# Loads begun singly, a conversion held in one layer, early products at a mixer's head, and a router's lead-in in a fixed order

## Chip, cores and metric

The kernel runs on one core of one Trainium2 chip. The metric is the device time of one execution in microseconds (us). The core has TensorE (PE in the rows, with PEld for its weight loads), VectorE (DVE), ScalarE (ACT), GpSimd (POOL) and SyncE (SP), which issues most of the DMAs.

## What is computed

The reference is a network for 256 tokens of width 1024 in float32: two hybrid layers, an RMS norm, a mixer of four branches, and a mixture of experts with a layer norm. Cut to its frame:

```python
def hybrid_layer(x, c, ...):                    # twice
    mod = silu(c) @ ada_w + ada_b               # six vectors that scale and shift
    h = rms_norm(x, norm_mix_g) * (1 + sc_m) + sh_m
    proj = h @ w_in                             # NA, MLA and GQA inputs, three gates
    o_na = neighborhood_attention(qa, ka, va, na_rpb)
    q_b = rms_norm(cq, mla_q_norm_g) @ mla_w_uq           # the up-projections
    kv_b = rms_norm(ckv, mla_kv_norm_g) @ mla_w_ukv
    o_mla, o_gqa = blocked_attention(...), blocked_attention(...)
    merged = sigmoid(ga) * (o_na @ w_br_na) + ...         # three branches
    x = x + g_m * (merged @ w_out)
    h = rms_norm(x, norm_ffn_g) * (1 + sc_f) + sh_f
    gate, up = split(h @ ffn_w_gate_up)
    return x + g_f * ((silu(gate) * up) @ ffn_w_down)

x = rms_norm(x, final_norm_g)
proj = x @ w_in                                 # mixer: four branches
y_a = rg_lru(a_in, ...)                         # a convolution, then a scan
y_b = gated delta rule on qkv, beta, decay      # "gdn"
y_c = stick-breaking attention; y_d = gated linear attention   # "sb", "gla"
x = layer_norm(a * x + merged @ w_out)
scores = sigmoid(x @ w_router)                  # 16 experts in 4 groups, top 2
x = layer_norm(a * x + sum over chosen experts of weight * expert(x))
```

## The kernel before

Activations stand transposed: features on the 128 partitions, the 256 tokens along the free axis, so that a tile of 1024 features is eight blocks of 128x256. Every large product is done at near float32 precision by three matmuls: each operand is kept as a high part (hi: tiles `wh`, `hh`) and a rest (lo: `wl`, `hl`), and `mm3` (or `blockT`, L195 to L197) issues hi x hi, lo x hi and hi x lo into the same PSUM bank.

A weight reaches PE in three steps. `raw` (L156) has SyncE load 1 MB into one of three raw slots (`wr`); `pieces` has ACT convert each half to the high part (L163) and DVE subtract it from the raw weight to give the rest (L170), each a pass of 128x1024. There are five slots for high parts and five for rests. A raw slot is free for the next load when its conversions and subtractions are done. `pieces` takes three switches: `s.behind` names an instruction after which the conversion must be placed, `s.hold` is a list of instructions after which the next subtractions must be placed, one each, and `s.defer` collects subtractions to be emitted later. Those are orders in the program's sequence, not waits on a value.

The order on each engine comes from a planner, which goes through the program in the order of the code, simulates the engines and lets an instruction pass others where its operands and slots are there. `s.after(a, b)` sets an order by hand. Every engine then works through its own list in order.

**Modulation (`ada`, L385; `tick`, L410).** The six vectors of a layer are sums over products of a row with weights: 8 loads of 512 KB a vector, issued by GpSimd (L405) into one of ten `big` slots, and for each one DVE pass with an accumulated sum (L398). The generator is advanced once per weight load (`tick`, called in `raw`), and with `pace` 2 it issues two loads and does two sums a tick; the sums run four loads behind. In each layer the loads of vectors 4, 3 and 2 begin at the two up-projection weights and go on through the twelve gate weights.

**Attention and up-projection (L735 to L815).** Neighbourhood attention's scores are computed; the exponentials (L134) run on ACT, the sums' reciprocals (L438) and the scaling (L440) on DVE. The program then takes the up-projections: `w_uq` and `w_ukv` are loaded and converted with `s.behind = evac`, the copy that empties a bank of values (L734). PE's products for the query heads are emptied by DVE into `qf` (L768). GpSimd copies keys (`kg`, L788), and the gate weights follow (`L_att.wr`, `L_gates.wr` in the rows: the label is that of the part which was last named), PE's gate products mixed with the attention's steps. After them come the branch products, whose banks DVE empties with L817, and the output product.

**The mixer's head (L1018, L1070, L1486).** `final_norm` ends the norm (`norm_end`, whose reciprocal root is done by `rsq` on ACT and one Newton step on DVE, L252 to L254), keeps the factor r in a slot for weight rests, and scales the input in eight blocks (L1028), each followed by its split into hi and lo (L237 on ACT, L238 on DVE). Two products don't wait for that: they take `s.z`, the input before the factor, and the factor is applied to the product: the two blocks of `rg` (L1487 to L1492, the second one's weight loaded there), and `misc` (L1070, a product of 128 columns, emptied with the factor at L1072). The six gdn products (L1076) use the normalised input; the first is block 2. PSUM banks are named: mm, s and t have two buffers, o and ad one.

**The router's lead-in (L1695 to L1850).** `out_norm` computes the output product by column block i and token half b, with the layer norm's statistics, and starts the router's product from it before the norm is applied. At the last block of each half it makes mr and u (L1715, L1716), and applies the norm in four quarters, each with two DVE passes (L1648, L1649). Then PE adds the carried input into four banks (L1735, `aI` times the normalised rows). `route` completes the scores (L1765), exponential, reciprocal, two rankings, `sel` (L1793); PE counts with `sel` (L1796 to L1799); DVE makes positions and the gather's matrix P (L1841); PE gathers the tokens of each expert (L1854) and goes on to the experts' products. The first expert weights are loaded ahead, and part of their subtractions deferred (`later`). `route_weights` loads `w_rt` at the start into a tile of its own.

## Time and profile before

| | us |
|---|---|
| median of 3 runs | 1578.55 (1578.36 to 1579.76) |
| profiled execution | 1578.81 |
| its span in the trace | 1577.1 |
| PE busy | 1515.9 (96%) |
| DVE busy | 1199.1 (76%) |
| ACT busy | 902.7 (57%) |
| GpSimd busy | 100.7 (6%) |
| mean granted clock of PE | 0.986 of full |

Busy shares are averages over many stages. PE is busy nearly all the time, so the places of interest are those in which it isn't: the table of stretches finds them, and the engines' rows in order of time tell what they waited for. A row of a timeline gives its start, its duration, the engine, the line, the operation, the tile written and those read, a count if like rows were joined, and in brackets the idle time of the engine ahead of it with what ended that.

### The profile page before, as it was taken

The numbers are of one execution on the slowest core, as the hardware profiler recorded it, in microseconds if no ns is written. First come the engines' busy times: TensorE is split into PE (matmuls) and PEld (weight loads), VectorE is DVE, ScalarE is ACT, GpSimd is POOL, SyncE is SP. The second block draws the span as 40 slices with busy tenths as digits, with TensorE's granted clock in tenths as the row PEclk, the third lists the DMA queues.
The fourth block names the chain that finished last, engine by engine and source line by source line (L and its number), as shares of the span: only waits on it lengthen the run. The fifth ranks groups of instructions, "written<-read, shape, count | busy, mean of one in ns | idle before, by whom it ended". The sixth has DMA issues, their size and how long they took to land.

```text
span 1577.1 us, 27664 instructions
## 1 busy us (share of the span) xinstructions
PE 1515.9 (96%) x11216; PEld 1397.5 (89%) x11216; DVE 1199.1 (76%) x1760; ACT 902.7 (57%) x1316; POOL 100.7 (6%) x173
## 2 busy tenths in 40 slices
PE   6999999999997999999998999999999899999996
PEld 5889999999986989999997989989999688888884
DVE  5899789776785997975558875566666798888896
ACT  5565555444563554644446662675555477777774
POOL 0211000000001110000000022122000000000000
PEclk9999999999998999999999999999999999999998
DMA  9879676876446876565554640335656499999992
GB/s 348 283 238 305 198 240 200 308 267 215 134 141 231 288 241 212 183 208 188 187 174 143 188 126 9 117 103 157 186 175 227 160 324 330 330 330 331 332 346 79
DMA packets 206197, 346.27 MB, mean 220 GB/s; under 512 B 6944, under 2 KB 175024, under 8 KB 193776
## 3 DMA queue, kind: packets, MB, share of 16 engines
q1 hardware_dynamic: 191040, 294.42, 56.0%
q0 software_dynamic: 12656, 46.16, 8.3%
q10 hardware_dynamic: 2368, 3.86, 0.7%
q8 instruction: 90, 1.47, 0.4%
q14 instruction: 43, 0.35, 0.1%
HBM read 343.36 MB, written 1.05 MB: 218 GB/s over the span
## 4 chain that ended last, share of the span: by engine, by line
PE 68%; issue 23%; DVE 4%; DMA 3%; ACT 2%; POOL 0%; ACTq 0%; DVEq 0%; POOLq 0%; SPq 0%
PE L_gu.mm L195 5%; PE L_gu.mm L197 5%; PE L_gu.mm L196 5%; PE L_att.mm L195 3%; PE L_att.mm L197 3%; PE L_att.mm L196 3%; PE M_merge.mm L197 2%; PE M_merge.mm L195 2%; PE M_merge.mm L196 2%; PE L_gu.s L196 2%; PE L_gu.s L195 2%; PE L_gu.s L197 1%; PE L_gu.t L197 1%; PE L_gu.t L196 1%; PE L_gu.t L195 1%
## 5 line engine op out<-in xcount | busy, mean ns | idle before, releaser
L197 PE MATMUL L_gu.mm<-L_fnorm.hh,L_gu.wl 128*128 128x256 f32 x640 | 179.0, 280 | 0.0
L196 PE MATMUL L_gu.mm<-L_fnorm.hl,L_gu.wh 128*128 128x256 f32 x640 | 178.8, 280 | 0.0
L195 PE MATMUL L_gu.mm<-L_fnorm.hh,L_gu.wh 128*128 128x256 f32 x640 | 178.1, 279 | 0.0
L170 DVE TENSOR_TENSOR E_gu.wl<-E_gu.wr,E_gu.wh 128x1024 fp32r<-128x1024 f32 x124 | 150.1, 1224 | 21.2 <-ACT E_gu.wh L163 16.8
L170 DVE TENSOR_TENSOR L_gu.wl<-L_gu.wr,L_gu.wh 128x1024 fp32r<-128x1024 f32 x84 | 102.7, 1224 | 70.8 <-ACT L_gu.wh L163 70.3
L163 ACT CAST E_gu.wh<-E_gu.wr 128x1024 fp32r<-128x1024 f32 x124 | 129.7, 1054 | 40.0 <-PE E_gu.mm L197 11.7
L163 ACT CAST L_gu.wh<-L_gu.wr 128x1024 fp32r<-128x1024 f32 x84 | 88.2, 1050 | 112.4 <-PE L_gu.mm L196 70.5
L195 PEld LDWEIGHTS L_gu.mm<-L_fnorm.hh,L_gu.wh 128*128 128x128 f32 x640 | 120.2, 188 | 0.4 <-ACT L_fnorm.hh L310 0.4
L197 PEld LDWEIGHTS L_gu.mm<-L_fnorm.hh,L_gu.wl 128*128 128x128 f32 x640 | 120.5, 188 | 0.0
L196 PEld LDWEIGHTS L_gu.mm<-L_fnorm.hl,L_gu.wh 128*128 128x128 f32 x640 | 120.0, 188 | 0.0
L398 DVE SCALAR_TENSOR_TENSOR ada.big<-ada.big,L_mlaup.crow 128x1024 f32<-128x1024 f32 x80 | 95.9, 1218 | 0.0
L163 ACT CAST L_down.wh<-L_down.wr 128x1024 fp32r<-128x1024 f32 x48 | 50.5, 1052 | 75.3 <-PE L_gu.mm L196 39.8
L170 DVE TENSOR_TENSOR L_down.wl<-L_down.wr,L_down.wh 128x1024 fp32r<-128x1024 f32 x48 | 58.4, 1224 | 38.3 <-ACT L_down.wh L163 38.3
L163 ACT CAST L_att.wh<-L_att.wr 128x1024 fp32r<-128x1024 f32 x44 | 46.3, 1052 | 66.2 <-PE L_att.mm L196 35.7
L170 DVE TENSOR_TENSOR E_down.wl<-E_down.wr,E_down.wh 128x1024 fp32r<-128x1024 f32 x64 | 75.7, 1223 | 5.1 <-ACT E_down.wh L163 4.9
L163 ACT CAST E_down.wh<-E_down.wr 128x1024 fp32r<-128x1024 f32 x64 | 66.3, 1057 | 15.7 <-PE E_down.mm L197 6.5
L170 DVE TENSOR_TENSOR M_merge.wl<-M_merge.wr,M_merge.wh 128x1024 fp32r<-128x1024 f32 (+1 forms) x50 | 48.2, 969 | 30.5 <-ACT M_merge.wh L163 30.5
L405 POOL DMA_DIRECT2D ada.big<-in_ada_t x80 | 42.2, 529 | 390.2 <-DVE ada.big L398 200.9
L163 ACT CAST M_merge.wh<-M_merge.wr 128x1024 fp32r<-128x1024 f32 (+1 forms) x50 | 41.9, 843 | 44.0 <-PE M_merge.mm L196 38.3
L197 PE MATMUL M_merge.mm<-fnorm.hh,M_merge.wl 128*128 128x256 f32 x208 | 59.2, 284 | 0.0
L195 PE MATMUL M_merge.mm<-fnorm.hh,M_merge.wh 128*128 128x256 f32 x208 | 58.1, 279 | 0.0
L196 PE MATMUL M_merge.mm<-fnorm.hl,M_merge.wh 128*128 128x256 f32 x208 | 57.8, 278 | 0.0
(982 smaller groups left out, 5392.0 us busy)
## 6 DMA issues: line engine op xcount, KB each, us to landing
L_gu.wr<-in_w_gu SPq DMA_DIRECT2D x42, 1024.0 KB, 5.1
ada.big<-in_ada_t POOLq DMA_DIRECT2D x80, 512.0 KB, 5.8
E_gu.wr<-in_wu SPq DMA_DIRECT2D x32, 1024.0 KB, 5.1
E_down.wr<-in_wd SPq DMA_DIRECT2D x32, 1024.0 KB, 5.4
E_gu.wr<-in_wg SPq DMA_DIRECT2D x30, 1024.0 KB, 5.0
L_att.wr<-in_w_in SPq DMA_DIRECT2D x22, 1024.0 KB, 6.1
L_down.wr<-in_w_dn SPq DMA_DIRECT2D x22, 1024.0 KB, 4.9
M_merge.wr<-in_w SPq DMA_DIRECT2D x13, 1024.0 KB, 5.3
```

The source lines that it names most:

```text
L163: c = s.nc.scalar.copy(hi, src).ins
L170: i = s.nc.vector.tensor_sub(lo, src, hi).ins
L195: mm(ps, ah, bh, start=first and fresh and k == 0, stop=False, skip_group_check=True)
L196: mm(ps, ah, bl, start=False, stop=False, skip_group_check=True)
L197: mm(ps, al, bh, start=False, stop=last and k == n - 1, skip_group_check=True)
L398: nc.vector.scalar_tensor_tensor(raw, raw, 0.5, s.crow, op0=ALU.mult, op1=ALU.mult, accum_out=sums[:, k:k + 1])
L405: s.tc.keep_in_program_order(nc.gpsimd.dma_start(raw, s.I["ada_t"][l, v, i % 8]))
```

## The change

It has six parts. `ada` takes a new argument `slow`: its first 4 steps give way after every load, and later ones after every second. The conversions of the up-projections are held behind the eviction in layer 0 only. `final_norm` loads the second `rg` weight ahead of the norm's end, and `w_misc` and the weight of gdn's block 2 behind it, their first three subtractions being placed after the Newton step; r gets a tile of its own, and two blocks are split at a time. gdn's block 2 is computed from the input before the factor, in bank t, as misc is, in bank s; `times_zr` applies the factor. A constant mask is computed from another one. In the router's lead-in the norm is applied in halves; for the second token half the second passes are placed by hand, one next to the exponential and one after `sel`, its carry products come after the counts, the copy of its rows is done in halves, and weight subtractions are placed after P. `w_rt` is loaded in the GLA stage, on GpSimd's queue, into a slot that another tile has used.

```diff
-        nc.vector.scalar_tensor_tensor(r, t, -3.0 * n, r, op0=ALU.add, op1=ALU.mult)
+        s.newton = nc.vector.scalar_tensor_tensor(r, t, -3.0 * n, r, op0=ALU.add, op1=ALU.mult).ins
...
-    def ada(s, vs, mods, pace, lag):
+    def ada(s, vs, mods, pace, lag, slow=0):
-            if i % pace == pace - 1:
+            if i < slow or (i - slow) % pace == pace - 1:
                 yield False
...
-        s.side = [s.ada([(l, v) for v in (4, 3, 2)], mods, 2, LAG[0])]
+        s.side = [s.ada([(l, v) for v in (4, 3, 2)], mods, 2, LAG[0], 4)]
-        s.behind = evac
+        s.behind = None if l else evac
...
     def final_norm(s, x):
-        r = s.t([128, 1024], "wl", WH, pool=s.w)[:, :256]
+        r = s.c.tile([128, 256], F32, name="zr")
+        s.ahead = s.ahead, s.load(s.I["w2"][:, 256:512], 8, 256)
         s.norm_end(out=r)
+        s.hold = [s.newton] * 3
+        s.ahead += s.load(s.I["w_misc"], 8, 128), s.load(s.I["w2"][:, OFF["gdn"] + 512:OFF["gdn"] + 768], 8, 256)
...
-            s.split(hi[:, k], lo[:, k], xf[:, k])
+            if k % 2:
+                s.split(*(v[:, k - 1:k + 1].rearrange("p a b -> p (a b)") for v in (hi, lo, xf)))
+    def times_zr(s, p):
+        t = s.t([128, 512], "b2", NB2)
+        v = lambda t: t.rearrange("p (a b) -> p a b", a=2)
+        s.nc.vector.tensor_tensor(v(t), v(p), s.zr.unsqueeze(1).to_broadcast([128, 2, 256]), ALU.mult)
+        return t
...
-        p = s.proj(0, s.z, 128, I["w_misc"])
+        p = s.proj(0, s.z, 128, s.ahead[2], "s")
-        for i, bank in ((2, "mm"), (3, "ad"), (0, "mm"), (1, "o"), (4, "mm"), (5, "ad")):
-            p = s.proj(OFF["gdn"] + 256 * i, x, bank=bank)
+        for i, bank in ((2, "t"), (3, "ad"), (0, "mm"), (1, "o"), (4, "mm"), (5, "ad")):
+            p = s.proj(OFF["gdn"] + 256 * i, *((s.z, 256, s.ahead[3]) if i == 2 else (x,)), bank=bank)
+            if i == 2:
+                p = s.times_zr(p)
...
-            nc.vector.tensor_tensor(s.v4(dm), s.v4(ps), C["mneg"]..., ALU.add)
+            nc.vector.scalar_tensor_tensor(s.v4(dm), C["ugt"]..., -1e30, s.v4(ps), op0=ALU.mult, op1=ALU.add)
...
         for i in range(2):
-            w = s.ahead if i == 0 else s.load(I["w2"][:, 256:512], 8, 256)
             pz = s.acc()
-            s.blocks(pz, w, s.z)
+            s.blocks(pz, s.ahead[i], s.z)
+            p = s.times_zr(pz)
...
         B = s.gla_decay(misc)
+        s.wr = s.t([128, 256], "misc", 1)[:, :128].rearrange("p (k n) -> p k n", k=8)
+        nc.gpsimd.dma_start(s.wr, s.I["w_rt"].rearrange("(k p) n -> p k n", p=128))
...
                     s.norm_stats(st, mv, r, ax[b], b)
+                    scaled(0)
...
-                    for q in range(4):
-                        c = slice(q * 256, (q + 1) * 256)
-                        s.norm_apply(x2, ax[b][:, c], mv, r, g, bb, b, c)
+                    scaled(1)
+                    if b:
+                        s.x2 = shifted
+                    else:
+                        for q in range(2):
+                            shifted(q)
...
-        for b in range(2):
+        def carried(b, i):
             for d in range(2):
                 j = nc.tensor.matmul(yp[2 * b + d], aI, x2[:, b, d * 512:(d + 1) * 512], ...).ins
                 s.after(j, i)
                 i = j
+        carried(0, last[0])
...
         s.fn(sc, u, AF.Exp, scale=-1.0)
+        s.x2(0)
...
+        s.after(s.x2(1), chosen)
...
-        s.after(nc.scalar.copy(xh[:, 1], x2[:, 1]).ins, s.load_ins)
+        s.after(nc.scalar.copy(xh[:, 1, :512], x2[:, 1, :512]).ins, s.load_ins)
...
             if g == 0:
+                nc.scalar.copy(xh[:, 1, 512:], x2[:, 1, 512:])
+                carried(1, at)
                 s.after(nc.vector.tensor_sub(xl[:, 1], x2[:, 1], xh[:, 1]).ins, i)
+                s.placed = i
...
         later, s.defer = s.defer, None
+        s.hold = [s.placed] * 2
...
         for sub in later:
-            sub()
+            s.after(sub().ins, s.placed)
```

`scaled(q)` is the first of the norm's two passes over columns 512q to 512q + 511, `shifted(q)` the second. `chosen` is the instruction that makes `sel`, `at` the last count, and `i`, where `s.placed` is set, the one that makes P.

## Rows read from the trace of the kernel before

**Rows 1.** the page's table of engines: busy time, share of the span, instructions:

```profile
PE 1515.9 (96%) x11216; PEld 1397.5 (89%) x11216; DVE 1199.1 (76%) x1760; ACT 902.7 (57%) x1316; POOL 100.7 (6%) x173
```

**Rows 2.** stretches: length, busy time of each engine, granted clock, DMA share, GB/s:

```profile
80.00:105.00 25.00, 23.00 (x158) 19.79 (x157) 24.19 (x48) 18.00 (x34) 4.70 (x10) 1.00 0.66 219
480.00:505.00 25.00, 13.28 (x98) 11.65 (x97) 11.01 (x22) 7.99 (x16) 5.72 (x12) 0.79 0.83 294
835.00:860.00 25.00, 19.21 (x137) 17.11 (x135) 23.48 (x59) 15.31 (x29) 0.00 (x0) 0.86 0.45 141
1235.00:1260.00 25.00, 18.36 (x98) 13.65 (x97) 21.55 (x61) 10.84 (x17) 0.64 (x2) 0.86 0.53 184
```

**Rows 3.** PE in order of time, layer 1's stall:

```profile
491.38 0.70 PE L426 MATMUL L_att.s<-L_naqkv.big 64*128 64x256 f32 x2
503.58 0.58 PE L195 MATMUL L_mlaup.mm<-L_lat.ch,L_mlaup.wh 128*128 128x256 f32 x1 [11.51 <-DVE L_mlaup.qf L768]
```

**Rows 4.** ACT, DVE, POOL and SP in order of time, the same stall:

```profile
499.98 1.04 ACT L163 CAST L_att.wh<-L_att.wr 128x1024 fp32r<-128x1024 f32 x1 [12.85 <-DMA L_att.wr<-in_w_in]
...
502.06 0.17 DVE L438 RECIPROCAL L_att.psum<-L_att.psum 128x2 f32<-128x2 f32 x1 [10.50 <-ACT L_att.b L134]
...
482.63 3.13 POOL L405 DMA_DIRECT2D ada.big<-in_ada_t  x6
...
483.92 12.70 SPq L156 DMA_DIRECT2D L_att.wr<-in_w_in  x3
```

**Rows 5.** DMAs from 482 to 500: queues; then issues, KB, us to landing:

```profile
q0 software_dynamic: 1152, 4.19, 62.3%
q1 hardware_dynamic: 1784, 1.81, 28.9%
...
ada.big<-in_ada_t POOLq DMA_DIRECT2D x8, 512.0 KB, 7.0
L_att.wr<-in_w_in SPq DMA_DIRECT2D x3, 1024.0 KB, 18.4
```

**Rows 6.** the page's DMA issues of the whole span, us to landing:

```profile
L_att.wr<-in_w_in SPq DMA_DIRECT2D x22, 1024.0 KB, 6.1
```

**Rows 7.** stretches, behind layer 1's stall:

```profile
496.00:508.00 12.00, 4.42 (x20) 4.41 (x21) 3.35 (x11) 4.83 (x14) 0.53 (x1) 0.50 0.76 248
```

**Rows 8.** DVE in order of time, router:

```profile
1244.74 0.87 DVE L1649 SCALAR_TENSOR_TENSOR M_out.x<-M_out.x,lnr,M_out.b 128x256 f32<-128x256 f32 x2
...
1246.55 1.22 DVE L170 TENSOR_TENSOR E_gu.wl<-E_gu.wr,E_gu.wh 128x1024 fp32r<-128x1024 f32 x1
```

**Rows 9.** PE in order of time, mixer's head:

```profile
848.62 0.39 PE L195 MATMUL M_gdn.ad<-fnorm.hh,M_gdn.wh 128*128 128x256 f32 x1 [1.50 <-ACT M_gdn.wh L163]
...
852.95 0.55 PE L195 MATMUL M_gdn.mm<-L_down.hh,M_gdn.wh 128*128 128x256 f32 x1 [3.83 <-DVE M_rg.b L1492]
```

**Rows 10.** DVE in order of time, mixer's head:

```profile
843.41 0.42 DVE L254 SCALAR_TENSOR_TENSOR fnorm.wl<-fnorm.b,fnorm.wl 128x256 f32<-128x256 f32 x1
...
852.12 1.28 DVE L1492 TENSOR_TENSOR M_rg.b<-M_rg.mm,fnorm.wl 128x512 f32<-128x512 f32 x2
```

**Rows 11.** stretches, layer 0's branch products:

```profile
200.00:225.00 25.00, 24.96 (x212) 24.76 (x211) 23.16 (x34) 12.88 (x17) 2.11 (x4) 1.00 0.78 254
```

**Rows 12.** stretches, behind the mixer head's waits:

```profile
853.00:860.00 7.00, 7.00 (x43) 5.79 (x43) 7.00 (x27) 4.95 (x10) 0.00 (x0) 0.77 0.56 185
```

**Rows 13.** PE in order of time, router:

```profile
1241.39 3.26 PE L1735 MATMUL M_ln.s<-M_out.x,M_out.b 128*128 128x512 f32 x4
...
1246.69 1.10 PE L1735 MATMUL M_ln.t<-M_out.x,M_out.b 128*128 128x512 f32 x2 [0.23 <-DVE score L1767]
1250.83 0.18 PE L1796 MATMUL E_route.o<-sel,M_out.b 128*128 128x32 bf16 x1 [3.04 <-DVE sel L1793]
...
1252.45 0.55 PE L1854 MATMUL E_gather.mm<-E_gather.P,M_out.hh 128*128 128x256 f32 x1 [1.38 <-DVE E_gather.P L1841]
```

**Rows 14.** stretches, block 0's carries:

```profile
1242.00:1244.00 2.00, 2.00 (x4) 0.56 (x2) 2.00 (x6) 0.46 (x2) 0.00 (x0) 0.50 0.01 4
```

More of the change, by code (lines that the diff above doesn't have):

```diff
@@ L933, in shape_constants2 @@
     o["ugt"] = (j > i)
-    o["mneg"] = np.where(i >= j, 0, -1e30)
     for b in (1, 2, 4, 8, 16, 32, 64):
@@ L1002, in proj @@
     def proj(s, col0, x, ncol=256, w=None, bank="mm"):
-        w = s.load(s.I["w2"][:, col0:col0 + ncol] if w is None else w, 8, ncol)
+        w = w or s.load(s.I["w2"][:, col0:col0 + ncol], 8, ncol)
         p = s.acc(bank)
@@ L1140, in gdn @@
             dm = s.t([128, 512], "b2", NB2)
-            nc.vector.tensor_tensor(s.v4(dm), s.v4(ps), C["mneg"].unsqueeze(1).to_broadcast([128, 4, 128]), ALU.add)
+            nc.vector.scalar_tensor_tensor(s.v4(dm), C["ugt"].unsqueeze(1).to_broadcast([128, 4, 128]), -1e30, s.v4(ps), op0=ALU.mult, op1=ALU.add)
             for h in range(4):
@@ L1486, in rglru @@
         for i in range(2):
-            w = s.ahead if i == 0 else s.load(I["w2"][:, 256:512], 8, 256)
             pz = s.acc()
-            s.blocks(pz, w, s.z)
-            p = s.t([128, 512], "b2", NB2)
-            v = lambda t: t.rearrange("p (a b) -> p a b", a=2)
-            nc.vector.tensor_tensor(v(p), v(pz), s.zr.unsqueeze(1).to_broadcast([128, 2, 256]), ALU.mult)
+            s.blocks(pz, s.ahead[i], s.z)
+            p = s.times_zr(pz)
             for j in range(2):
@@ L1643, in norm_tiles @@
         return s.t([128, 2, 2, 6], tag + "st", 1), s.t([128, 2, 2], tag + "mv", 1), s.t([128, 2], tag + "r", 1)
-    def norm_apply(s, out, z, mv, r, g, b, t, c):
-        nc = s.nc
-        nc.vector.scalar_tensor_tensor(out[:, t, c], z, mv[:, t, 0:1], g[:, c], op0=ALU.subtract, op1=ALU.mult)
-        nc.vector.scalar_tensor_tensor(out[:, t, c], out[:, t, c], r[:, t:t + 1], b[:, c], op0=ALU.mult, op1=ALU.add)
     def out_norm(s, m, xf):
@@ L1714, in block, with scaled, shifted @@
                     s.norm_stats(st, mv, r, ax[b], b)
+                    half = lambda q: (x2[:, b, q * 512:(q + 1) * 512], ax[b][:, q * 512:(q + 1) * 512], g[:, q * 512:(q + 1) * 512], bb[:, q * 512:(q + 1) * 512])
+                    def scaled(q):
+                        o, z, gq, _ = half(q)
+                        return nc.vector.scalar_tensor_tensor(o, z, mv[:, b, 0:1], gq, op0=ALU.subtract, op1=ALU.mult).ins
+                    def shifted(q):
+                        o, _, _, bq = half(q)
+                        return nc.vector.scalar_tensor_tensor(o, o, r[:, b:b + 1], bq, op0=ALU.mult, op1=ALU.add).ins
+                    scaled(0)
                     nc.vector.scalar_tensor_tensor(mr[:, b:b + 1], mv[:, b, 0:1], -1.0, r[:, b:b + 1], op0=ALU.mult, op1=ALU.mult)
                     nc.vector.scalar_tensor_tensor(u[:, b * 16:b * 16 + 16], s.csbw[:, :16], mr[:, b:b + 1], s.csbw[:, 16:], op0=ALU.mult, op1=ALU.add)
-                    for q in range(4):
-                        c = slice(q * 256, (q + 1) * 256)
-                        s.norm_apply(x2, ax[b][:, c], mv, r, g, bb, b, c)
+                    scaled(1)
[4 more added lines that the diff above has]
+                            shifted(q)
         ws, last = {}, [None]
@@ L1729, in out_norm @@
                 nc.vector.tensor_sub(xl[:, 0], x2[:, 0], xh[:, 0])
-        i = last[0]
         yp = [s.acc(t) for t in "sstt"]
-        for b in range(2):
+        def carried(b, i):
             for d in range(2):
@@ L1737, in out_norm @@
                 i = j
-        return x2, xh, xl, yp, s.route(pr[:, :32], u, r)
+        carried(0, last[0])
+        return x2, xh, xl, yp, s.route(pr[:, :32], u, r) + (carried,)
     def route_weights(s):
-        s.wr = s.c.tile([128, 8, 16], F32, name="wrt")
-        s.late(s.nc.gpsimd.dma_start(s.wr, s.I["w_rt"].rearrange("(k p) n -> p k n", p=128)))
         s.rb = s.c.tile([128, 16], F32, name="rb")
@@ L1792, in route @@
         sel = s.c.tile([128, 32], BF16, name="sel")
-        nc.vector.scalar_tensor_tensor(v4(sel), v4(r), 2.0, gm.unsqueeze(2).to_broadcast([128, 8, 4]), op0=ALU.is_lt, op1=ALU.mult)
+        chosen = nc.vector.scalar_tensor_tensor(v4(sel), v4(r), 2.0, gm.unsqueeze(2).to_broadcast([128, 8, 4]), op0=ALU.is_lt, op1=ALU.mult).ins
         pp = s.acc("o")
@@ L1798, in route @@
         for b in range(2):
-            nc.tensor.matmul(pp[:, 32:48], s.onesb[:, 0], sel[:, 16 * b:16 * b + 16], start=False, stop=b == 1, skip_group_check=True)
+            at = nc.tensor.matmul(pp[:, 32:48], s.onesb[:, 0], sel[:, 16 * b:16 * b + 16], start=False, stop=b == 1, skip_group_check=True).ins
+        s.after(s.x2(1), chosen)
         pos, mx = (s.c.tile([128, n], F32, name=m) for n, m in ((16, "pos"), (1, "most")))
@@ L1808, in route @@
         nc.vector.tensor_reduce(mx, n8, axis=AX.X, op=ALU.max)
-        return sel, sc, pos, mx
+        return sel, sc, pos, mx, at
     def combine(s, sel, sc):
@@ L1823, in moe @@
         ident = s.cst["ident"]
-        sel, sc, pos, mx = rt
+        sel, sc, pos, mx, at, carried = rt
         s.table(SILU)
         LAB[0] = 'E_gather.'
-        s.after(nc.scalar.copy(xh[:, 1], x2[:, 1]).ins, s.load_ins)
+        s.after(nc.scalar.copy(xh[:, 1, :512], x2[:, 1, :512]).ins, s.load_ins)
         f = lambda t: t.rearrange("p a b -> p (a b)")
```

## Prediction

> **What bounds the kernel.** I read the engine table first: TensorE (PE) is busy 1515.9 of 1577.1 us [rows 1], so 61.2 us is all that a better order can give back, apart from matmuls that ran at a low clock. Next comes the table of stretches, and in it the few of 25 us in which PE is far from full: 13.28, 19.21 and 18.36 us busy, which leaves 11.72, 5.79 and 6.64, and a lesser one in layer 0 with 23.00, which leaves 2.00 [rows 2]. Together 26.2 of the 61.2 us. All four lie where the diff works, and in the three large ones the granted clock is under 1 as well. In each I then read the engines in order of time for the wait that ended last. Elsewhere PE is close to full, and what VectorE (DVE) or ScalarE (ACT) saves there is worth nothing.
>
> **Layer 1, the softmax stall.** PE ends its score products at 491.38 + 0.70 = 492.08 and next works at 503.58, after 11.51 idle, released by VectorE's qf (L768) [rows 3]. What ended last stands further back: DVE's reciprocal at 502.06 had waited 10.50 for the exponentials, and these were queued on ACT behind a conversion that had waited 12.85, to 499.98, for a 1 MB gate weight to land. SyncE had issued that weight at 483.92, once a conversion had given a raw slot back; GpSimd had issued six modulation loads of 512 KB in one burst from 482.63 [rows 4]. From 482 to 500 eight modulation loads landed in 7.0 us at the median and three gate weights took 18.4 [rows 5]; over the whole run such gate weights take 6.1 [rows 6].
>
> The change works on both causes in this layer. Without `behind` the up-projection's conversion goes as soon as its weight and a slot are there, no longer after an eviction, so the raw slot comes back sooner. How much sooner the trace of before can't show: nothing, or so much that the weight lands ahead of the burst. And with the first four modulation loads begun one to a tick, three or four are begun by that point and not six. With 6.1 us to land, a weight issued at 483.92 is there at 490.0 even if it is issued no earlier, and its conversion is over at 491.1 (1.04). DVE had stopped at 502.06 - 10.50 = 491.56, so its input to the exponentials was ready. From the end of the conversion to PE's restart it took 503.58 - 499.98 - 1.04 = 2.6; so PE restarts near 491.6 + 2.6 = 494.2, and some 2.1 of the 11.5 remain, about what layer 0 loses in its stretch [rows 2]. That is 9.4. The matmuls behind the stall ran at a granted clock of 0.50 (1.2 GHz): 4.42 us of work from 496 to 508 [rows 7], half of which, 2.2, comes back where PE doesn't stand so long. 9.4 + 2.2 = 11.6; **I take 11**, for weights that are still somewhat late. Bounds: 13.7 (11.5 + 2.2) if nothing is left, 6 if the burst is only halved (rival C).
>
> **Layer 0** keeps `behind`; its loads begin singly too. 2.00 us is all there is; I take 0.4, between 0 and 1.5. Price of beginning singly: the last sums come two weight ticks later (16 for 14), four sums a layer, each a pass of 128x1024, 1.22 by the nearest row of that size [rows 8]. I cost them at nothing, the gate products hide them; without that cover they cost 4 x 1.22 = 4.9 a layer (rival D). No load is added.
>
> **Mixer head.** PE runs dry at 848.62 (1.50) and at 852.95 (3.83, until DVE's L1492 has freed the bank that the misc product needs) [rows 9]. The norm's last Newton step is at 843.41; L1492 comes only at 852.12, behind gains, subtractions and weight subtractions [rows 10]; DVE is busy 23.48 of 25 [rows 2]. The change gives PE products that need no normalised input: misc in bank s, 24 matmuls, which was there but blocked, and gdn's block 2 in bank t, 48 that came later. A full stretch holds 212 such matmuls in 24.96 us [rows 11], 0.118 each; 72 x 0.118 = 8.5, so PE has work from about 847.1 to 855.6. Is DVE ready by then? From 843.8 it owes three held weight subtractions (3 x 1.22), eight gains (8 x 0.42, by the Newton step's 128x256), four subtractions and two scalings of 512 (6 x 0.65, L1492 took 1.28 for two): 3.7 + 3.4 + 3.9 = 11.0, so 854.8. It just fits, and the convolutions wait too. Gain: 5.3 of idle, and the half clock behind it, 7.00 us of work at a mean of 0.77 [rows 12], 1.6; together 6.9. **I take 5**, for a wait of about 2 on the normalised input; bounds 0 (DVE sets the pace, rival B) and 7. The scaling that gdn's block adds costs DVE 0.65, in the stretch counted. zr in a tile of its own gives one lo slot to the weights; three more weights are loaded ahead on SyncE's queue, which pushes the next ones behind the release of their slots: in the wait of 2. The mask that is computed in place of a constant lengthens two operations by a few hundredths: 0.1.
>
> **Router.** PE waits 3.04 for sel at 1250.83 and 1.38 for the gather's P at 1252.45 [rows 13]. In DVE's order a weight subtraction of 1.22 stands ahead of the reciprocal at 1246.55, and before it quarter passes of block 1's normalisation, two in 0.87, which the scores don't need [rows 8]. The change holds such subtractions until P is placed (this one and one like it from further ahead, 2.44), and moves the four second passes (4 x 0.44 = 1.8) as two halves, one beside the exponential, one behind sel. Onto the path come about 0.7 for a scaling ahead of the scores and 0.4 each where a half outlasts what hides it (halves of 512 at 0.65 to 0.7). 2.4 + 1.8 - 1.5 = 2.7 earlier at P, 3.1 at sel. But block 1's carry products, 2 x 1.10 at full clock [rows 13], now stand between sel and the gather: from 1250.83 - 3.1 = 1247.7 and the counts to 1250.1, where P is ready at 1249.8. So the gather starts 2.3 earlier. **I take 2.1.** Bounds: 4 if the gather also runs at the full level, -1 if the held subtractions, three or more of 1.22 now behind P, delay the casts of what was gathered. The load of w_rt goes from the start to the GLA stage on GpSimd's queue: one issue, about 0.5 by the burst (six in 3.13) [rows 4], ahead of GLA's products there; it is needed only after the merges. Nothing.
>
> Here the clock counts. Block 0's four carry rows took 3.26, at a granted clock of 0.50 after PE had had gaps, block 1's four took 2.20 [rows 13, 14]. Behind some 4 us of idle the moved ones may meet the low level themselves; then they end 1.1 later, and the gather behind them comes to the full level sooner, which gives about as much back. That is why the term stays. The Trainium skill's page "TensorE: Matmul & The Clock Gate", Part 1, What's actually happening, speaks against this move: the throttled state is the default, and activity releases it. By that alone the term would be about 1 and the time 1 us longer; the row of that stretch agrees with it, and no row shows these products in their new place.
>
> **The sum.** 11 + 0.4 + 5 + 2.1 = 18.5, less 0.1 for the mask. The profiled execution is its span and 1.7 around it, 1578.81, 0.3 over the median of the runs. 1578.8 - 18.4 = 1560.4, said as **1560**.
>
> **Rivals.**
> A, the forecast: 1560. Chance 0.57.
> B, DVE sets the pace in the head and the router, where it was busy 23.48 and 21.55 of 25 [rows 2] and its work is moved, not taken out: only layers 0 and 1 give, 1578.8 - 11.4 = 1567. For it: the 11.0 us that only just fit. Against: 8.5 us of PE work that waits for no DVE. 0.15.
> C, the burst still meets the gate weights, because GpSimd then sends what has gathered. With four loads in flight for eight, 2.1 of 4.19 MB are spared, at the 6.0 MB in 18 us of that stretch [rows 5] 6.3 us, and the clock gives nothing: 6, and 7.4 elsewhere: 1578.8 - 13.4 = 1565. 0.12. The Trainium skill's page "DMA: Bandwidth & Descriptors", Queues, rings and completion order, says that a DMA engine takes the queues with work in turn, a packet at a time. By that the queue of larger packets gets the larger share, as it does in rows 5, and C would give back somewhat more.
> D, slower: the modulation sums arrive in the branch stage. There DVE is busy 23.16 of 25 with what frees PE's banks, and PE 24.96 [rows 11], so a sum put there is paid in full. It decides from eight sums a layer behind the branch's start: 8 x 1.22 = 9.8, and 2 for the clock, in both layers, 23.6: more than the 18.4 gained, 1584. Against: by ticks only four come later. 0.08.
> E, the diff leaves the order in these stretches as it was, since most of it isn't written by hand: 1577. 0.08.
>
> **Chances and range.** A, B and C are faster by over 0.2% (3.2 us, about what a measurement of this kernel can tell from no change): 0.84. E is the same, 0.08; D is slower, 0.08. Range: A with its terms at 13, 0.5, 7 and 4 gives 1554, at 9, 0, 3 and 1 gives 1566; B and C lie within 1568, both together at 1578.8 - 6.4 = 1572. **1554 to 1572** leaves out D, E and a little.
>
> **What would show it.** Layer 1: no wait of over 4 us on ACT for L_att.wr from 480 to 510, and a clock of 1.00. Head: misc and gdn's block 2 running to about 855, then one wait of 2 at most. Router: sel 3 us sooner after the output projection's last product, block 1's carries right behind it. Against it: ACT at a weight for 10 us (C, E), DVE full and PE waiting for it behind 847 (B), L398 among the branch products (D).

## The result and the profile after

The changed kernel takes 1558.1 us (median of 4 runs, 1557.59 to 1559.87), the kernel before beside it 1579.15 (4 runs, 1578.36 to 1581.09). The ratio is 0.9867, with an interval of 0.985 to 0.9884: faster by 1.3%, clear of the noise, 1.9 us below the 1560 of the forecast and inside its range. The profiled execution took 1558.08, its span 1556.4.

The page's table of engines of the changed kernel, and its table of stretches for the places of rows 2, each at the changed kernel's own times; the columns are those of rows 2:

```profile
PE 1510.9 (97%) x11216; PEld 1392.8 (89%) x11216; DVE 1196.5 (77%) x1749; ACT 901.5 (58%) x1313; POOL 101.7 (7%) x173
```

```profile
80.00:105.00 25.00, 22.97 (x156) 19.57 (x155) 24.05 (x46) 17.99 (x34) 3.91 (x9) 1.00 0.62 205
480.00:505.00 25.00, 24.52 (x188) 21.80 (x188) 19.44 (x37) 15.09 (x32) 6.25 (x13) 1.00 0.88 301
825.00:850.00 25.00, 24.06 (x194) 22.86 (x195) 22.75 (x51) 18.16 (x28) 0.00 (x0) 1.00 0.61 183
1220.00:1245.00 25.00, 18.98 (x93) 13.33 (x92) 21.08 (x55) 11.67 (x20) 0.71 (x2) 0.93 0.59 221
```

PE's idle time has gone from two of the three large places: 13.28 busy of 25 became 24.52 in layer 1, 19.21 became 24.06 in the head, both at a clock of 1.00. The router still has 6.0 idle, and layer 0 is as it was [rows 1, 2]. PE's busy time fell by 5.0 for the same 11216 matmuls, with a mean granted clock of 0.994 where it was 0.986.

Where the 20.7 us of span went is best read from landmarks: the start of the first matmul into a tile that both kernels have, in PE's rows in order of time. The stretches between them, the change against the kernel before in us (start-up ends at layer 0's first L_naqkv.mm, the lead-in is layer 1's norm and modulation up to the same tile there, the stall ends at the first L_gates.mm; the head runs from the first L_gu.mm of layer 1 to M_sbin.mm, the router from the output product's last statistics to E_gu.ad, the tail from there to PE's last matmul; rest: the two stretches between):

| kernel | start-up | layer 0 | lead-in | stall | head | router | tail | rest | all |
|---|---|---|---|---|---|---|---|---|---|
| the change | 1.22 | -0.16 | -1.22 | -10.98 | -7.30 | -1.67 | -0.55 | -0.11 | -20.77 |
| conversion freed alone | -0.15 | -0.12 | -1.24 | -11.76 | 0.41 | 0.15 | -0.04 | 0.02 | -12.73 |
| single loads alone | -0.21 | -0.23 | -1.19 | -1.36 | -0.02 | -0.02 | -0.07 | 0.31 | -2.79 |
| three ticks later alone | -0.46 | -0.11 | -0.51 | -4.98 | 0.00 | 0.08 | -0.05 | -0.30 | -6.33 |
| change, loads in pairs | 0.23 | -0.11 | -1.21 | -11.76 | -7.26 | -2.11 | -0.48 | -0.03 | -22.73 |
| change, no early gdn | 0.24 | -0.10 | -0.25 | -10.98 | -2.43 | -2.11 | -0.34 | 0.08 | -15.90 |
| change, subtractions not held | -0.33 | -0.18 | -0.69 | -10.98 | -7.29 | 2.32 | 0.01 | -0.01 | -17.15 |
| change, once more | 0.50 | -0.20 | -0.16 | -11.00 | -7.27 | -3.25 | -0.46 | -0.05 | -21.89 |

Start-up and lead-in are scatter: programs with the start of the kernel before lie at -0.46 to 2.26, those with the start of the change at -0.33 to 2.58, and the lead-in lies at -1.24 to 1.26. Between programs with the same code the stall repeats to 0.1, the head to 0.4 (the 0.41 of the second line has the head of the kernel before), the router only to 1.6, for a reason that comes below.

### The profile page after: what moved, and what is told of

Its sections match the earlier page's. It is cut to its first block, busy times and chain, and to the rows that moved or that the text cites. A ratio compares the mean times of both kernels' runs of the same rounds, so it can differ in the third digit from the quotient of the medians.

```text
span 1556.4 us, 27649 instructions
## 1 busy us (share of the span) xinstructions
PE 1510.9 (97%) x11216; PEld 1392.8 (89%) x11216; DVE 1196.5 (77%) x1749; ACT 901.5 (58%) x1313; POOL 101.7 (7%) x173
## 4 chain that ended last, share of the span: by engine, by line
PE 68%; issue 23%; DVE 4%; ACT 2%; DMA 1%; POOL 0%; ACTq 0%; POOLq 0%; DVEq 0%; SPq 0%
PE L_gu.mm L195 5%; PE L_gu.mm L196 5%; PE L_gu.mm L197 5%; PE L_att.mm L195 3%; PE L_att.mm L197 3%; PE L_att.mm L196 3%; PE M_merge.mm L197 2%; PE M_merge.mm L195 2%; PE M_merge.mm L196 2%; PE L_gu.s L196 2%; PE L_gu.s L195 2%; PE L_gu.s L197 2%; PE L_gu.t L197 1%; PE L_gu.t L196 1%; PE L_gu.t L195 1%
## 5 line engine op out<-in xcount | busy, mean ns | idle before, releaser
L398 DVE SCALAR_TENSOR_TENSOR ada.big<-ada.big,L_mlaup.crow 128x1024 f32<-128x1024 f32 x80 | 96.3, 1219 | 0.0
L170 DVE TENSOR_TENSOR L_att.wl<-L_att.wr,L_att.wh 128x1024 fp32r<-128x1024 f32 x44 | 53.4, 1220 | 8.4 <-ACT L_att.wh L163 8.2
```

The source lines that it names most:

```text
L170: i = s.nc.vector.tensor_sub(lo, src, hi).ins
L398: nc.vector.scalar_tensor_tensor(raw, raw, 0.5, s.crow, op0=ALU.mult, op1=ALU.mult, accum_out=sums[:, k:k + 1])
```

## The experiments

**The layer 1 stall: which of the two causes?** The theory of the prediction was that both parts work together, the earlier conversion and the smaller burst. The rivals: the conversion alone does it, or the burst alone does. Four kernels tell them apart. The first is the kernel before with the conversion freed in layer 1 and nothing else:

```diff
-        s.behind = evac
+        s.behind = None if l else evac
```

> The kernel before with one edit: in layer 1 the up-projection's conversion is no longer held behind the eviction. Theory 1, late issue: the first gate weight is requested some 9 us sooner, lands ahead of the burst of modulation loads, and ACT waits under 4 us for it; the stall of 11.5 us shrinks to 0 to 2 and the time falls by 11 to 13, to 1566 to 1568. Theory 2, burst alone: the weights still meet six modulation loads, a stall of 6 or more stays, 1572 to 1575.

It took 1566.17, and its stall is 11.76 shorter: the whole of it. The second is the kernel before with its loads begun singly and the conversion still held:

```diff
-        s.side = [s.ada([(l, v) for v in (4, 3, 2)], mods, 2, LAG[0])]
+        s.side = [s.ada([(l, v) for v in (4, 3, 2)], mods, 2, LAG[0], 4)]
```

> The kernel before with one edit: modulation loads begun singly for the first four steps, in both layers. If beginning singly is one of the two causes taken away, as the prediction has it, the burst at 482.6 is three or four loads and the stall falls to about 5: 1572 to 1574. The rival, from the trace of the changed kernel, where five loads still leave in one burst: the burst is one load shorter, a little over 1 us at most is gained, 1577 to 1580.

It took 1576.09, the stall 1.36 shorter, about what the rival said. The third begins layer 1's modulation loads three ticks later, the conversion still held:

```diff
         raws = []
+        for _ in range(wait):
+            yield False
...
-        s.side = [s.ada([(l, v) for v in (4, 3, 2)], mods, 2, LAG[0])]
+        s.side = [s.ada([(l, v) for v in (4, 3, 2)], mods, 2, LAG[0], 3 if l else 0)]
```

> The kernel before with one edit: in layer 1 the modulation loads begin three weight ticks later, so that the burst is one or two loads; the conversion stays held. Theory burst: the gate weight that is requested at 484 lands in about 6 us, at 490, and the stall shrinks to 2 or 3, 1567 to 1570. Theory late issue alone: the stall stays above 8, 1576 or more. Six sums come later, which may cost up to 5 behind the branch's start.

It took 1572.49, the stall 4.98 shorter: between the two theories. ACT, POOL, SP and PE in order of time, of the conversion freed alone, then of the single loads alone and of the later loads alone; "x6" counts joined rows:

```profile
486.42 1.05 ACT L163 CAST L_att.wh<-L_att.wr 128x1024 fp32r<-128x1024 f32 x1
...
481.38 3.14 POOL L405 DMA_DIRECT2D ada.big<-in_ada_t  x6
...
473.50 54.81 SPq L156 DMA_DIRECT2D L_att.wr<-in_w_in  x8
```

```profile
495.48 1.04 ACT L163 CAST L_att.wh<-L_att.wr 128x1024 fp32r<-128x1024 f32 x1 [9.97 <-DMA L_att.wr<-in_w_in]
...
481.00 2.62 POOL L405 DMA_DIRECT2D ada.big<-in_ada_t  x5
...
499.07 0.58 PE L195 MATMUL L_mlaup.mm<-L_lat.ch,L_mlaup.wh 128*128 128x256 f32 x1 [8.64 <-DVE L_mlaup.qf L768]
```

```profile
494.07 1.04 ACT L163 CAST L_att.wh<-L_att.wr 128x1024 fp32r<-128x1024 f32 x1 [8.00 <-DMA L_att.wr<-in_w_in]
...
481.56 2.10 POOL L407 DMA_DIRECT2D ada.big<-in_ada_t  x4
...
497.66 0.58 PE L195 MATMUL L_mlaup.mm<-L_lat.ch,L_mlaup.wh 128*128 128x256 f32 x1 [6.66 <-DVE L_mlaup.qf L770]
```

With the conversion freed, the burst of six is still there, and ACT waits for no weight at all: the gate weights are requested from 473.50 on, 7.9 us ahead of the burst. With the conversion held, the wait follows what GpSimd has sent: 12.85 behind six loads [rows 4], 9.97 behind five, 8.00 behind four. The burst isn't all of it, since single loads follow it while the weight is still on its way. GpSimd's queue from the weight's request to its landing, of the kernel before (483.92 to 499.96), the single loads alone (482.29 to 495.46) and the later loads alone (482.85 to 494.05): packets, MB, share of the 16 engines:

```profile
q0 software_dynamic: 1145, 4.17, 67.7%
...
q0 software_dynamic: 858, 3.12, 63.7%
...
q0 software_dynamic: 711, 2.59, 60.5%
```

That is about eight loads, six and five. All queues together moved 5.98, 4.88 and 4.07 MB in these 16.04, 13.17 and 11.20 us, at 373, 371 and 363 GB/s: the weight is late by the bytes that land with it, at a rate that hardly changes. So what GpSimd has sent is what makes a late weight so late, and the conversion is what makes it late. That is rival C's mechanism, though in the change no wait comes of it: the third gate weight, requested at 488.26 behind its burst, takes 8.8, and ACT waits for no weight. The Trainium skill's page "DMA: Bandwidth & Descriptors", Queues, rings and completion order, has queues served in turn, packet by packet; that the queue of the larger packets (4.17 MB in 1145, against 1.80 in 1769 on the weight's) moved more agrees with it in sign, and no run here isolates packet size.

The fourth is the changed kernel with loads in pairs again (the argument 4 made 0), which asks what beginning singly is worth in it:

> The changed kernel with one part undone: modulation loads begun in pairs again. If the freed conversion alone removes the stall, the time stays within 1 us of the changed kernel, 1557 to 1559. If beginning singly is needed as well, 4 to 6 us of the stall return, 1562 to 1564.

It took 1556.11. The stall is 11.76 shorter than in the kernel before, for 10.98 in the change: beginning singly costs 0.78, in this pair and in every program of either kind. No wait explains it (ACT waits for no weight in either). PE's small attention products stand in another order among the large ones: from start to next start, the 64 of L457 into L_att.o take 8.69 us in the change and 8.11 here, the 64 of L448 7.93 and 7.78. That is 0.73 of the 0.78.

**Layer 0: why is the conversion still held there?** The changed kernel with `s.behind = None` in both layers:

> The changed kernel with one edit: the conversion isn't held in layer 0 either. In layer 1 of the changed kernel the freed conversion stands 1 us ahead of an eviction, whose wait on PE grew from 0.68 to 1.50. Theory: layer 0 has no late gate weight, so it only pays the same 0.8: 1558 to 1560. Rival: the first gate weight comes sooner there too and 0.5 to 1 us of layer 0's 2 us of waits go.

It took 1563.98, worse than theory and rival both; layer 0 is 6.62 longer than in the kernel before. Its ACT, PE and SP rows in order of time:

```profile
74.84 1.04 ACT L163 CAST L_mlaup.wh<-L_mlaup.wr 128x1024 fp32r<-128x1024 f32 x1 [4.65 <-DMA L_mlaup.wr<-in_w_uq]
75.80 0.58 ACT L734 COPY L_naqkv.big<-L_naqkv.mm 128x512 f32<-128x512 f32 x1
...
76.43 0.58 PE L195 MATMUL L_gqaqkv.mm<-L_lat.hh,L_gqaqkv.wh 128*128 128x256 f32 x1 [5.31 <-ACT L_naqkv.big L734]
...
67.21 0.37 SPq L156 DMA_DIRECT2D L_mlaup.wr<-in_w_uq  x1
```

In layer 0 the up-projection's weight is requested only at 67.21. A conversion that is free to go early stands in ACT's list ahead of an eviction, waits 4.65 for its weight, and the eviction, which was ready, and PE behind it wait along (5.31, where the change has 0.68). That is 4.6 of the 6.62; most of the rest is half clock, a granted 0.50 over 3.57 us of PE's work from 76 to 80. In layer 1 the same weight is there (requested at 457.12, converted at 472.02), so there the early place costs little. The same edit is a gain of 11.8 in one layer and a loss of 6.6 in the other.

**The head: are both early products needed?** The changed kernel with gdn's block 2 computed from the normalised input again, in bank t, misc still early:

```diff
-        s.hold = [s.newton] * 3
-        s.ahead += s.load(s.I["w_misc"], 8, 128), s.load(s.I["w2"][:, OFF["gdn"] + 512:OFF["gdn"] + 768], 8, 256)
+        s.hold = [s.newton]
+        s.ahead += s.load(s.I["w_misc"], 8, 128),
...
-            p = s.proj(OFF["gdn"] + 256 * i, *((s.z, 256, s.ahead[3]) if i == 2 else (x,)), bank=bank)
-            if i == 2:
-                p = s.times_zr(p)
+            p = s.proj(OFF["gdn"] + 256 * i, x, bank=bank)
```

> The changed kernel with gdn's block 2 computed from the normalised input again, in bank t, its weight loaded in its turn; misc stays early in bank s. In the trace of the changed kernel misc ran late (at 854.8) and gdn's block 2 alone filled the gap, 834.8 to 840.7. Theory: that block is the cover, 5.7 us of products; without it PE waits for the normalised input, which DVE has two weight subtractions (2.4 us) sooner, so 2 to 4 us are lost, 1560 to 1562. Rival: misc, 2.8 us of products, moves up and is cover enough, within 1 us of the changed kernel.

It took 1562.99, and the head gains 2.43 in place of 7.30. PE in order of time:

```profile
835.74 0.38 PE L196 MATMUL M_gdn.t<-fnorm.hl,M_gdn.wh 128*128 128x256 f32 x1 [0.35 <-DVE fnorm.hl L238]
...
839.27 0.58 PE L197 MATMUL M_gdn.t<-fnorm.hh,M_gdn.wl 128*128 128x256 f32 x1 [3.03 <-DVE M_gdn.wl L170]
```

and the stretch behind it, from 839 to 850:

```profile
839.00:850.00 11.00, 10.73 (x69) 10.06 (x70) 11.00 (x37) 6.99 (x12) 0.00 (x0) 0.75 0.44 127
```

So gdn's block 2 carries 4.9 of the 7.3: 2.4 as idle time (gaps of 3.36 in the head for 0.93 in the change) and, by the rest, 2.5 as half clock. Misc, though allowed early in this program too, doesn't fill the gap. But PE waits only 0.35 for the normalised input here, and 3.03 for the rest of the weight, whose subtraction no longer stands right behind the Newton step (838.00, behind the gains). The edit takes away the early product and that place together, so it isn't shown which of the two is worth the 4.9: the normalised input with the subtraction held early wasn't run. The other half of the question is the bank alone: the kernel before with misc in bank s.

```diff
-        p = s.proj(0, s.z, 128, I["w_misc"])
+        p = s.proj(0, s.z, 128, I["w_misc"], "s")
```

> The kernel before with one edit: the misc product goes into bank s. If the bank was all that kept it from the gap, its 24 matmuls (2.8 us) run within the waits of 1.50 and 3.83 us and the head is 2.5 to 3.5 shorter, 1575 to 1577. If the waits were for the normalised input, PE waits for the next product instead, and the head is shorter by under 1.

It took 1584.61, where a gain was expected (4.2 of what it lies above the kernel before is scatter at the start, in the lead-in and the router; the head itself is 1.57 longer). PE in order of time:

```profile
852.46 0.42 PE L195 MATMUL M_gdn.ad<-fnorm.hh,M_gdn.wh 128*128 128x256 f32 x1 [1.85 <-ACT M_gdn.wh L163]
...
856.80 0.55 PE L195 MATMUL M_gdn.mm<-fnorm.hh,M_gdn.wh 128*128 128x256 f32 x1 [3.70 <-DVE M_rg.b L1492]
```

Both waits of rows 9 are there again, 1.85 for 1.50 and 3.70 for 3.83, the second ahead of a gdn product, which now is what wants bank mm. Misc, in a bank of its own, runs only at 869.60. The wait belonged to the bank and to the place of L1492 in DVE's list, and not to misc.

**The router: what holds the gather?** The profile of the change showed a wait that the prediction hadn't seen, DVE's P behind PE's moved carries. The theory for it: `aI` lies in a buffer of the stage's pool, which passes to P's tile, so P can't be written before the last carry has read it. Rival: P is late because of its place in DVE's list. The changed kernel with `aI` in r's lasting tile, free by then:

```diff
-        aI = s.t([128, 512], "b2", NB2)[:, :128]
+        aI = s.zr[:, :128]
```

> The changed kernel with one edit: the scaled identity of the carry products lies in the tile of the norm's factor, which outlives the stage, and no longer in a stage buffer whose memory P gets. Theory: P's wait of 2.66 us for the carry products goes, the gather starts right behind them (0.6 sooner), and DVE's casts come 2.7 sooner, so that PE's waits of 1.06 and 0.25 behind the gather go too: 1.5 to 2 us less, 1555.5 to 1557. Rival: the carries, 3.6 us at half clock, and DVE's held subtractions set the end anyway: under 0.6.

It took 1559.84, of which 2.39 are the start-up's. DVE and PE in order of time, of the change, then of this kernel, and last DVE's P in the change's second profile:

```profile
1231.41 0.76 DVE L1860 TENSOR_TENSOR E_gather.P<-pos,cst 128x256 fp32r<-128x256 f32 x2 [2.66 <-PE M_ln.t L1753]
...
1227.62 0.18 PE L1814 MATMUL E_route.o<-sel,M_out.b 128*128 128x32 bf16 x1 [2.82 <-DVE sel L1811]
1227.73 3.58 PE L1753 MATMUL M_ln.t<-M_out.x,M_out.b 128*128 128x512 f32 x4
1231.94 0.36 PE L1876 MATMUL E_gather.mm<-E_gather.P,M_out.hh 128*128 128x256 f32 x1 [0.62 <-issue]
```

```profile
1230.44 0.76 DVE L1860 TENSOR_TENSOR E_gather.P<-pos,cst 128x256 fp32r<-128x256 f32 x2
...
1229.21 0.18 PE L1814 MATMUL E_route.o<-sel,M_out.b 128*128 128x32 bf16 x1 [1.19 <-DVE sel L1811]
1229.31 1.96 PE L1753 MATMUL M_ln.t<-M_out.x,zr 128*128 128x512 f32 x4
1231.07 0.87 PE L1876 MATMUL E_gather.mm<-E_gather.P,M_out.hh 128*128 128x256 f32 x4
...
1238.75 0.63 PE L197 MATMUL E_gu.o<-E_gather.wh,E_gather.xgl 128*128 128x512 f32 x1
```

```profile
1230.15 0.76 DVE L1860 TENSOR_TENSOR E_gather.P<-pos,cst 128x256 fp32r<-128x256 f32 x2 [1.03 <-PE M_ln.t L1753]
```

The wait is gone and the gather starts right behind the carries, so it was the buffer. From sel's product to the gather it takes 1.86 us and not 4.32, but 1.6 of that is the clock: block 1's carries took 3.58 there and 1.96 here. In the change's second profile they took 1.96 as well, P waited 1.03, and the way was 2.69; so the buffer is worth 0.8 at the gather. At the end of the stretch no gain is shown: the router is 2.22 shorter than in the kernel before, between the change's two profiles (1.67 and 3.25), with a low phase on the first expert's products (0.63 each at 1238.75).

Next, with that edit kept, the first half of block 1's carries goes ahead of the counts, where PE waits for sel anyway (`first()` is `carried(1, j, (0,))`, with j block 0's last carry):

```diff
         s.x2(0)
+        first()
...
-                carried(1, at)
+                carried(1, at, (1,))
```

> As e6_lasting_ai, and the carry product of the first half of block 1 goes ahead of the counts, into PE's wait for sel. Theory: it takes some 1.0 of idle time, and only one product of 1 to 1.8 us stands between sel and the gather: 1.5 to 2 less than e6_lasting_ai, 1553.5 to 1555.5. Rival: the gather then meets the low clock that the carries had borne, and half of that comes back: 0.5 to 1 less than e6_lasting_ai.

Timed against the kernel before it took 1558.34 (4 runs, 1554.47 to 1560.57), ratio 0.9855 with an interval of 0.9831 to 0.9878; its router is 3.11 shorter than that of the kernel before. Beside the run with the lasting `aI` alone that is 0.9, less than the router's scatter, and the median is that of the change: whether the early half helps isn't told apart. And the changed kernel without the held subtractions:

```diff
-        s.hold = [s.placed] * 2
...
-            s.after(sub().ins, s.placed)
+            sub()
```

> The changed kernel with one part undone: the expert weights' subtractions are no longer placed behind P. Theory of the prediction: they stand in the way of the scores again, 2.44 of DVE time, so that sel comes 1.2 to 2.4 later than in the changed kernel (5.69 after the output norm's last product there), and P with it. Rival: P waits for the carry products anyway, so later scores cost the gather less than 1, and the casts behind the gather come sooner, which gives that back.

It took 1561.67; the router is 2.32 longer than before the change. DVE and PE in order of time:

```profile
1222.50 1.17 DVE L168 TENSOR_TENSOR E_gather.wl<-E_gather.wr,E_gather.wh 128x1024 fp32r<-128x1024 f32 x1
...
1225.94 1.21 DVE L170 TENSOR_TENSOR E_gu.wl<-E_gu.wr,E_gu.wh 128x1024 fp32r<-128x1024 f32 x1
...
1230.43 0.19 PE L1814 MATMUL E_route.o<-sel,M_out.b 128*128 128x32 bf16 x1 [4.87 <-DVE sel L1811]
```

From the output product's last statistics to sel it takes 9.43 here, 5.69 in the change, 10.35 before. The holds give 3.74 of the 4.66, the halves 0.92. Two subtractions stand here between those statistics and sel, and a third of 1.22 a little ahead, at 1219.74: together 3.6.

**All that the runs pointed to, beside the change.** The changed kernel with loads in pairs, the lasting `aI` and the early half, and in the same comparison the changed kernel once more:

> Three edits of the changed kernel that single runs favoured: modulation loads in pairs again, the scaled identity in the tile that outlives the stage, one carry product ahead of the counts. By the stretches of those runs: 0.8 less in layer 1, 1 to 1.5 less in the router, 1555.5 to 1556.5 at the median, against the changed kernel run beside it. Rival: a few us of scatter in the start and the clock behind sel cover that: within 1 us of the changed kernel, intervals that overlap.

> The changed kernel itself, timed in the same rounds as e9_pairs_half_early so that the two can be compared: 1557.5 to 1560, a ratio of 0.985 to 0.988 to the kernel before.

The first took 1555.21 (5 runs, 1554.12 to 1557.34), ratio 0.9848, interval 0.9835 to 0.9862; the second 1557.1 (4 runs, 1555.29 to 1557.2), ratio 0.9856, interval 0.9841 to 0.9871. The 1.9 between the medians is what their parts promise (0.78 in the stall, about 1 in the router), but the intervals overlap: that it is faster than the change isn't shown.

## Why the prediction came out as it did

**Layer 1: 11 forecast, 10.98 measured, though the step was wrong in four terms that cancel: luck.** The changed kernel's POOL, SP, ACT and PE rows in order of time, to be read beside rows 3 and 4:

```profile
482.72 2.61 POOL L405 DMA_DIRECT2D ada.big<-in_ada_t  x5
...
474.84 50.38 SPq L156 DMA_DIRECT2D L_att.wr<-in_w_in  x8
...
487.76 1.05 ACT L163 CAST L_att.wh<-L_att.wr 128x1024 fp32r<-128x1024 f32 x1
...
473.60 0.39 PE L195 MATMUL L_gqaqkv.mm<-L_norm.hh,L_gqaqkv.wh 128*128 128x256 f32 x1 [1.50 <-ACT L_naqkv.big L734]
491.20 0.38 PE L195 MATMUL L_mlaup.mm<-L_lat.ch,L_mlaup.wh 128*128 128x256 f32 x1 [0.21 <-DVE L_mlaup.qf L768]
```

and the DMA view of the changed kernel from 470 to 482, ahead of the burst (KB each, us to landing):

```profile
L_att.wr<-in_w_in SPq DMA_DIRECT2D x2, 1024.0 KB, 5.3
```

The failed step is "the change works on both causes". I had the gate weight requested at 483.92 as before and spared only its long landing. In fact the freed conversion gives the raw slot back early enough to request it at 474.84, 9.1 us sooner, and it lands in 5.3 us before the burst begins. The prediction named this as possible ("or so much that the weight lands ahead of the burst") and didn't take it. Term by term: the idle time that was to remain at 2.1 is 0.1 (PE's L426 products end at 492.80 and the next matmul starts at 492.90), which gives 11.4; the half clock behind the stall gave back 1.2 and not 2.2, since the work from the restart to the last product ahead of the gates (503.58 to 508.01 in the kernel before) is 4.43 there and 3.21 in the change; the early conversion stands ahead of an eviction, and PE's wait for that, 0.68 before, is 1.50, which costs 0.8; and beginning singly costs 0.8. 11.4 + 1.2 - 0.8 - 0.8 = 11.0. Five loads were begun in the burst for the "three or four" I had counted; by then it made no wait.

**Layer 0: 0.4 forecast, 0.2 or nothing measured.** It lies within its bounds, but programs that leave layer 0 as it was (conversion freed alone, three ticks later alone) read 0.1 shorter too, so that a gain isn't shown. That `behind` has to stay there is shown.

**Rival D, the sums.** The last sum L398 of the changed kernel's layer 1 stands just ahead of its first branch eviction L817, and PE is full behind it; DVE in order of time, and the stretch:

```profile
588.31 1.22 DVE L398 SCALAR_TENSOR_TENSOR ada.big<-ada.big,L_mlaup.crow 128x1024 f32<-128x1024 f32 x1
...
591.30 0.69 DVE L817 SCALAR_TENSOR_TENSOR L_branch.b<-L_att.big,L_branch.mm 128x512 f32<-128x512 f32 x1
```

```profile
590.00:615.00 25.00, 25.00 (x214) 25.00 (x213) 23.36 (x37) 12.09 (x15) 2.47 (x5) 1.00 0.76 252
```

The later sums fit: this one starts 3.0 us ahead of the eviction and ends 1.8 ahead, and in layer 0 the last stands at 192.42 with the first eviction at 195.41. In the run with loads three ticks later the last sum (598.44) did come behind the first eviction (597.19), and the stretch from the gates on was no longer for it; so one sum in the branch stage cost nothing there, where the rival had it "paid in full".

**Head: 5 forecast, 7.30 measured, above my bound of 7.** The term that was mis-sized is DVE's readiness. DVE and PE in order of time, of the change:

```profile
831.38 0.43 DVE L254 SCALAR_TENSOR_TENSOR zr<-fnorm.b,zr 128x256 f32<-128x256 f32 x1
831.73 3.49 DVE L170 TENSOR_TENSOR fnorm.wl<-fnorm.wr,fnorm.wh 128x1024 fp32r<-128x1024 f32 x3
841.84 0.69 DVE L1039 TENSOR_TENSOR M_rg.b<-M_rg.mm,zr 128x512 f32<-128x512 f32 x1
...
834.84 0.27 PE L195 MATMUL M_gdn.t<-L_down.hh,fnorm.wh 128*128 128x256 f32 x1
840.50 0.28 PE L195 MATMUL M_gdn.ad<-fnorm.hh,M_gdn.wh 128*128 128x256 f32 x1
845.05 0.39 PE L197 MATMUL M_gdn.ad<-fnorm.hh,M_gdn.wl 128*128 128x256 f32 x1 [0.94 <-DVE M_gdn.wl L170]
854.76 0.39 PE L195 MATMUL M_gdn.s<-L_down.hh,fnorm.wh 128*128 128x256 f32 x1
```

I counted 11.0 us of DVE work from the Newton step to the first normalised product. PE takes the first split input 9.1 us behind it (840.50 - 831.38) and without a wait: products begin on the blocks that are split while DVE is at the others, and the scalings of rg, which I had put ahead, come after the gains (841.84). With the early product left out PE began on normalised blocks at 835.00, 3.5 behind the Newton step of that run, so that PE never had to wait for the whole 11.0. PE needs only gdn's block 2, 5.7 us, to bridge that; misc, which I had running beside it to about 855, comes 14 us later, at 854.76. What is left is one wait of 0.94 for a weight's rest, where I had taken off 2 for the normalised input. By idle time and clock: gaps in PE's rows from the first L_gu.mm to M_sbin.mm sum to 5.73 before and 0.93 after, so 4.8; and the granted clock was 0.77 over 2.67 us of busy time from 845 to 853 and over 7.00 behind [rows 12], 1.00 after, so 9.67 x 0.23 = 2.2. That is 7.0 of the 7.3. My reading of the second wait of rows 9 was half wrong: it is the wait for a bank and for L1492, and the run with misc's bank alone shows that it stays where it was.

**Router: 2.1 forecast, 1.67 measured in this profile and 3.25 in the next.** Both parts of the sum were off. Sel comes 4.66 earlier and not 3.1: three subtractions stood ahead of it where I had counted two (2.44), and the run without the holds puts 3.74 on them. What follows sel eats more than I took: P waited for the carries through the buffer of `aI`, a wait that no row before could show and that I could have read from the code, 2.66 in the change, 1.03 in its second profile. The clock question that I left open is answered by those two profiles of the same code: block 1's carries ran at the low level in the one (the table of stretches, changed kernel) and at the full one in the other (PE in order of time, second profile):

```profile
1229.00:1231.00 2.00, 2.00 (x3) 0.40 (x2) 0.00 (x0) 0.00 (x0) 0.00 (x0) 0.50 0.00 0
```

```profile
1223.28 3.58 PE L1753 MATMUL M_ln.s<-M_out.x,M_out.b 128*128 128x512 f32 x4
1227.99 0.18 PE L1814 MATMUL E_route.o<-sel,M_out.b 128*128 128x32 bf16 x1 [1.13 <-DVE sel L1811]
1228.09 1.96 PE L1753 MATMUL M_ln.t<-M_out.x,M_out.b 128*128 128x512 f32 x4
```

In the first, block 0's carries took 1.96, PE then waited 2.82 for sel, and block 1's took 3.58, all of it on the path; in the second block 0's took the low phase, in time that PE would have spent waiting for sel (its wait is 1.13 and not 2.82). The difference, 3.58 - 1.96 = 1.6, is the whole of the router's scatter. The Trainium skill's page "TensorE: Matmul & The Clock Gate", Part 1, What's actually happening, has the throttled state as the default that activity releases; the first profile agrees with that warning, at 1.6 where I had priced it at 1.1. In the second the same products run at the full level, so the order of the code alone doesn't decide it; what does is open.

**The mask, the w_rt load, the added scaling.** The mask and the new place of the w_rt load lie in the rest (-0.11), so that the 0.1 for the mask isn't told from nothing. The old place of that load lies in the start-up, whose scatter covers it, and the added scaling is in the head's sum.

**The rivals.** B is out: DVE stays as busy in the head (24.49 of 25 from 835 to 860) and PE there doesn't wait for it but for 0.94. C is out in the change, though its mechanism is real (the two runs with the conversion held). D and E are out by the rows above. The sum, 18.4 forecast and 20.8 measured, is off by the head's 2.3 and by 0.55 in the tail, which no experiment takes apart; in the other terms misses cancel.

## What to carry to other kernels

When a load is late, look first for what kept its slot from being given back, and only then at what else is on the queues: here one conversion placed behind an eviction delayed a request by 9 us, and removing that left the competing burst in place without a wait for it. A conversion in an engine's list is only as free as the load it waits for: placed early it helps where its weight has landed and blocks all that is queued behind it where it hasn't, so the same edit has to be judged layer by layer. Where a product is moved past another step, ask what memory it reads and who gets that memory next, for that wait isn't in any trace of before.

## What the runs showed of the hardware

The low clock level falls on other work from run to run of the same program, and whether it costs depends on whether that work is on the path: four carries of 512 columns took 3.58 or 1.96 us. In the changed kernel's first profile the matmuls from 21.15 to 22.21 lasted 0.41 us each, at starts 0.21 apart, where 0.28 and 0.12 are usual, while the granted clock of that stretch reads 1.00; so that column alone doesn't tell the level in so short a stretch. A weight of 1 MB that landed in 5.3 us ahead of the burst took 16.04, 13.17 and 11.20 behind it, when 4.17, 3.12 and 2.59 MB of the other queue landed with it, at 363 to 373 GB/s in all: as long as those bytes take. An instruction that waits for its load holds back ready ones behind it on its engine (4.65 us on ACT, 5.31 on PE). What makes the start-up differ by up to 3 us between profiles is open too.
